# A projection done alone: both weight pieces taken at once, all wide products with hi before all products with lo

## The chip, the cores and the metric

The kernel runs on one core of one Trainium2 chip. The metric is device time in microseconds (us) of one launch, the median of several runs. Before the change it is 2928.85 us (3 runs, 2928.5 to 2928.92). One more execution was taken with the hardware profiler; it took 2928.61 us, and its profile spans 2926.8 us.

## What is computed

The reference is a two-layer decoder trunk over 256 tokens of width 2048, in float32. Layer 0 mixes with a convolution group and a differential-attention group that share one input and one output projection, layer 1 with a short gated convolution. After its mixer each layer cross-attends with 4 heads of 512 into 256 memory tokens, and applies an MLP of width 8192 with squared ReLU. Cut to what matters here:

```
x = x + even_mixer(rms(x))  or  x + odd_mixer(rms(x))   # in: D -> 5*1024 or 3*2048; out: 2048 -> 2048
x = x + softmax((rms(x) @ wq) @ (mem @ wk).T) @ (mem @ wv) @ wo
x = x + square(relu(rms(x) @ w1)) @ w2                  # 2048 -> 8192 -> 2048
```

Nearly all the work is `act @ weight` with 256 rows of `act`, and each weight is used once.

## The kernel before

**Split numbers.** Every float32 operand is split in two: `hi`, rounded to the format that TensorE takes in one pass, and `lo`, what is left of it. A product is hi\*hi + lo\*hi + hi\*lo. Activations lie in `Act` objects: for each of 16 chunks of 128 channels, 256 columns of hi and 256 columns of lo side by side. `act.both(k)` is all 512 columns, `act.hi(k)` the first 256.

**Weights.** `weights(src)` (lines 152 to 165) brings one piece of 128 x 1024: SyncE issues the transfer into `raw` (5 buffers), ScalarE casts it to `whi` (line 163, 3 buffers), VectorE subtracts to get `wlo` (line 164, 3 buffers). A projection to 128 output channels reads 16 chunks, so two such pieces, `g = 0` and `g = 1`, of 8 blocks of 128 x 128 each.

**A projection alone.** `proj(src, act)` does one projection with one PSUM bank `mm` (4 buffers) through `proj_group`. In its wide form each piece is handled by `wide_piece` (lines 173 to 182): the hi blocks times `act.both` (512 columns: hi\*hi in the left half of the bank, hi\*lo in the right), then the lo blocks times `act.hi` (256 columns, left half). In the last piece the eighth hi block is kept back and closes the bank. So TensorE gets, for one projection, 8 products of 512 columns, 8 of 256, 7 of 512, 8 of 256, 1 of 512. Afterwards ScalarE copies the right half and VectorE adds it to the left (`summed`, lines 205 to 210), or VectorE adds both halves to the residual (`residual`, line 324). The narrow form (`wide=False`, products of 256 columns alone) serves the convolution inputs and the memory keys; `proj_rows` serves the values; `proj_group` with 3 or 4 sources serves the first output columns of `even_out` and `xo`.

**Who calls proj in its wide form.** The q and k of the differential attention (16), `even_out` (13), `odd_in` (48), `odd_out` (16), the cross-attention's q (32) and `xo` (24), and the MLP (256).

**The order of the work.** The framework orders each engine's instructions from its own plan, mostly by their order in the program. Two things are fixed by hand. While `strict[0]` is set (even mixer, and the cross-attention from its first query chunk to its first four output columns), all products go to TensorE in the program's order (`ordered(i, "pe")`). The `wlo` subtractions and the convolution taps on VectorE keep the program's order too. Work of the attention is placed by due times that are counted in calls of `weights`: `stage(delay, fn)` notes `fn` for `delay` calls later, and each call of `weights` first runs what is due (`run_stages`, line 154) and then counts itself:

```
run_later(rate[0], calls[0])
run_stages(calls[0])
calls[0] += 1
```

In the cross-attention (lines 642 to 710), a head's four query chunks are projected with `proj`, scaled and split into `xq` (lines 698 to 701), and then `stage(X0, scores)` with `X0, X1, X2 = 1, 2, 1`. `scores` does 24 products `sx` of 256 columns (for each half of the rows four chunks i, each with q hi, q lo, q hi), and the softmax; `turn` transposes 2 calls later; `heads_out` multiplies with the values 1 call after that. The differential attention has the delays `D0, D1, D2, D3 = 2, 3, 2, 2` for scores, transposes, output and the mean of squares; its heads come in pairs, two wide projections a head, followed by two pairs of narrow projections (`gated`).

Of the kernel before, what the change touches and what calls it, by code (L numbers as in the profile page):

```python
# [10 lines left out]
F32 = mybir.dt.float32  # L11
# [6 lines left out]
P = 128  # L18
D = 2048
S = 256  # L20
# [25 lines left out]
def trunk(ctx: ExitStack, tc: tile.TileContext, d):  # L46
# [11 lines left out]
    ps_mm = ctx.enter_context(tc.tile_pool(name="ps_mm", bufs=4, space=bass.MemoryType.PSUM))  # L58
# [3 lines left out]
    def f(ap):  # L62
        return ap.bitcast(F32)
# [55 lines left out]
    def ordered(i, token):  # L119

        tc.stamp_issue_order_token(i.ins, token)
# [7 lines left out]
    def run_later(n, upto):  # L129
        while n and background and background[0][0] <= upto:  # L130
            background.pop(0)[1]()
            n -= 1

    def run_stages(upto):
        while True:
            due = [e for e in stages if e[0] <= upto]
            if not due:
                return
            stages.remove(due[0])
            due[0][1]()  # L140

    def mm(*a, **k):
        i = T.matmul(*a, **k)  # L143
        if strict[0]:
            ordered(i, "pe")
# [6 lines left out]
    def weights(src):  # L152
# [3 lines that stand above are left out]
        raw = wraw.tile([P, 1024], F32, tag="raw", name="raw")  # L156
        hi = wspl.tile([P, 1024], F32R, tag="whi", name="whi")
        lo = wspl.tile([P, 1024], F32R, tag="wlo", name="wlo")
        n = 512 if calls[0] == 1 else 1024
        for i in range(0, 1024, n):  # L160
            o = slice(i, i + n)
            nc.sync.dma_start(out=raw[:, o], in_=src[:, o])
            A.copy(hi[:, o], raw[:, o])  # L163
            ordered(V.tensor_tensor(lo[:, o], raw[:, o], f(hi[:, o]), op=ALU.subtract), "lo")  # L164
        return hi, lo

    def block(ps, hi, lo, act, k, first, last):

        mm(ps, hi, act.hi(k), start=first, stop=False)
        mm(ps, hi, act.lo(k), start=False, stop=False)  # L170
        mm(ps, lo, act.hi(k), start=False, stop=last)

    def wide_piece(ps, hi, lo, act, k, first, last):


        w = [slice(j * P, (j + 1) * P) for j in range(8)]
        for j in range(7 if last else 8):
            mm(ps, hi[:, w[j]], act.both(k + j), start=first and j == 0, stop=False)
        for j in range(8):
            mm(ps[:, :S], lo[:, w[j]], act.hi(k + j), start=False, stop=False)  # L180
        if last:
            mm(ps, hi[:, w[7]], act.both(k + 7), start=False, stop=True)

    def proj_group(srcs, act, order=(0, 1), wide=True):


        pp = [ps_mm.tile([P, 512], F32, tag="mm", name="mm")[:, :(2 * S if wide else S)] for _ in srcs]
        for g in order:
            if g == order[-1] and len(srcs) > 1:
                run_stages(END)  # L190
            for src, ps in zip(srcs, pp):
                hi, lo = weights(src[:, g * 1024:(g + 1) * 1024])
                first, last = g == order[0], g == order[-1]
                if wide:
                    wide_piece(ps, hi, lo, act, g * 8, first, last)
                    continue
                for j in range(8):
                    w = slice(j * P, (j + 1) * P)
                    block(ps, hi[:, w], lo[:, w], act, g * 8 + j, first and j == 0, last and j == 7)
        return pp  # L200

    def proj(src, act, wide=True):
        return proj_group([src], act, wide=wide)[0]

    def summed(ps):
# [145 lines left out]
    def even_mixer():  # L351
# [37 lines left out]
        def qk(c, hl, name, sign):  # L389
            t = summed(proj(w[2 * NA + c], xa))  # L390
            V.scalar_tensor_tensor(t, t, sign, r, op0=ALU.mult, op1=ALU.mult)
            A.copy(hl[:, 0], t)
            V.tensor_tensor(hl[:, 1], t, f(hl[:, 0]), op=ALU.subtract)
            return hl
# [94 lines left out]
        def gated(c):  # L489
            pv = proj(w[c], xa, wide=False)  # L490
            av = tmp32("av")
            V.tensor_tensor(av, pv, r, op=ALU.mult)
            pg = proj(w[NA + c], xa, wide=False)
            ag = tmp32("ag")
            V.tensor_tensor(ag, pg, r, op=ALU.mult)
            A.activation(ag, ag, AF.Sigmoid)
            V.tensor_tensor(a[:, c], av, ag, op=ALU.mult)
            i = c * CK
            def tap(c=c, i=i, j=CK - 1):
                s = CK - 1 - j  # L500
                if not s:
                    ordered(V.tensor_scalar(cv[:, c], a[:, c], col("conv_a_w", i + j), col("conv_a_b", c),
                                            op0=ALU.mult, op1=ALU.add), "lo")
                else:
                    ordered(V.scalar_tensor_tensor(cv[:, c, s:], a[:, c, :S - s], col("conv_a_w", i + j),  # L505
                                                   cv[:, c, s:], op0=ALU.mult, op1=ALU.add), "lo")

            def total(c=c):
                if c == 0:
                    V.tensor_copy(lsum, cv[:, 0])  # L510
                else:
                    V.tensor_tensor(lsum, lsum, cv[:, c], op=ALU.add)

            for j in range(CK - 1, -1, -1):
                later(lambda tap=tap, j=j: tap(j=j))
            later(total)
# [60 lines left out]
        for c, ps in enumerate(proj_group([d["even_out"][c] for c in range(3)], cat, (1, 0))):  # L577
            residual(c, ps, nxt, nss, "xat0")
# [63 lines left out]
    def cross(l, xa, ss, kmem):  # L642
# [62 lines left out]
        for c, ps in enumerate(proj_group([d[f"xo{l}"][c] for c in range(4)], oa)):  # L705
            residual(c, ps, nxt, nss, f"mlp{l}")
# [96 lines left out]
```

## Time and profile before

| quantity | before |
|---|---|
| median of 3 runs | 2928.85 us |
| the profiled execution's own time | 2928.61 us |
| its span in the profile | 2926.8 us |
| mean granted TensorE clock | 0.998 |
| TensorE matmul (PE) busy | 2907.2 us, 99% |
| TensorE weight load (PEld) busy | 2583.8 us, 88% |
| VectorE (DVE) busy | 2000.0 us, 68% |
| ScalarE (ACT) busy | 1456.8 us, 50% |
| DMA | 540.12 MB, mean 185 GB/s |

PE and PEld are two rows for the same engine: PE the products, PEld the loads of the 128 x 128 block, which run ahead of them. Products are pipelined, so the time that one product costs isn't its listed duration but the distance from its start to the start of the next one; where below a number is called a pitch, this is meant. In a timeline the columns are start (us), duration of the group, engine, line, operation, output<-inputs, number of instructions, and in brackets the engine's idle time before it with what ended it.

### The profile page before, as it was taken

How to read it: one execution, taken by the hardware profiler on the slowest of the kernel's cores; microseconds unless marked ns; L12 is line 12 of the kernel's file. 1: busy time of each engine (PE TensorE's matmuls, PEld its weight loads, DVE VectorE, ACT ScalarE, POOL GpSimd, SP SyncE). 2: the span in 40 equal slices, each digit the busy share in tenths (PEclk: the TensorE clock that was granted, in tenths of full speed). 3: DMA queues.
4: the chain of work that ended last, by engine and by line, in shares of the span. 5: the costliest groups of instructions: out<-in, count | busy, mean ns of one | idle time of the engine just before them, and what ended most of it. 6: DMA issues, size and time to landing. Idle time of an engine off the chain costs nothing.

```text
span 2926.8 us, 44172 instructions
## 1 busy us (share of the span) xinstructions
PE 2907.2 (99%) x17304; PEld 2583.8 (88%) x17304; DVE 2000.0 (68%) x3132; ACT 1456.8 (50%) x2133; POOL 3.9 (0%) x20
## 2 busy tenths in 40 slices
PE   9999999999999999999999999999999999999998
PEld 7999988898888888888888899888988888888887
DVE  7899987767666656666777764467676666566665
ACT  6665455555544535445544443455555445354453
POOL 0000000000000000000000000000000000000000
PEclk9999999999999999999999999999999999999999
DMA  7454565545565665666655655655455656656564
GB/s 249 163 191 167 180 187 188 171 151 178 184 191 187 190 187 187 189 190 190 182 192 197 202 191 187 192 189 170 142 188 183 191 188 189 189 190 188 188 188 136
DMA packets 150401, 540.12 MB, mean 185 GB/s; under 512 B 16688, under 2 KB 16816, under 8 KB 150192
## 3 DMA queue, kind: packets, MB, share of 16 engines
q1 hardware_dynamic: 150192, 537.30, 58.0%
q8 instruction: 136, 2.23, 0.3%
q14 instruction: 73, 0.60, 0.1%
HBM read 535.13 MB, written 2.10 MB: 184 GB/s over the span
## 4 chain that ended last, share of the span: by engine, by line
PE 99%; DVE 0%; DMA 0%; ACT 0%; issue 0%; DVEq 0%; SPq 0%; ACTq 0%
PE mm L143 89%; PE mmr L143 8%; PE pox L143 1%; PE sx L143 1%; PE nmb L143 0%; PE sc L143 0%; PE nmr L143 0%; PE po L143 0%; DVE x L741 0%; PE ptx L148 0%; DMA x<-xT 0%; PE ptd L148 0%; ACT xn L254 0%; DVE x L324 0%; DVEq L798 0%
## 5 line engine op out<-in xcount | busy, mean ns | idle before, releaser
L163 ACT CAST whi<-raw 128x1024 fp32r<-128x1024 f32 (+1 forms) x1009 | 1060.3, 1051 | 829.4 <-PE mm L143 702.2
L164 DVE TENSOR_TENSOR wlo<-raw,whi 128x1024 fp32r<-128x1024 f32 (+1 forms) x1009 | 1233.6, 1223 | 278.4 <-ACT whi L163 260.5
L143 PE MATMUL mm<-xn,whi 128*128 128x512 f32 (+1 forms) x4096 | 997.5, 379 | 0.0
L143 PEld LDWEIGHTS mm<-xn,whi 128*128 128x128 f32 x4096 | 724.7, 189 | 115.6
L143 PE MATMUL mm<-xn,wlo 128*128 128x256 f32 x3840 | 572.9, 282 | 0.0
L143 PEld LDWEIGHTS mm<-xn,wlo 128*128 128x128 f32 x3840 | 537.8, 190 | 34.7
L143 PE MATMUL mm<-hid,whi 128*128 128x512 f32 x2048 | 514.1, 392 | 0.0
L143 PEld LDWEIGHTS mm<-hid,whi 128*128 128x128 f32 x2048 | 368.9, 189 | 65.9
L208 ACT COPY sum<-mm 128x256 f32<-128x256 f32 x224 | 83.4, 372 | 533.0 <-PE mm L143 532.8
L324 DVE TENSOR_TENSOR x<-x,mm 128x256 f32<-128x256 f32 x384 | 161.5, 421 | 265.9 <-PE mm L143 259.2
L209 DVE TENSOR_TENSOR sum<-mm,sum 128x256 f32<-128x256 f32 x224 | 95.0, 424 | 313.2 <-ACT sum L208 312.7
L143 PEld LDWEIGHTS mm<-hid,wlo 128*128 128x128 f32 x2048 | 279.4, 190 | 19.9
L143 PE MATMUL mm<-hid,wlo 128*128 128x256 f32 x2048 | 285.6, 282 | 0.0
L143 PE MATMUL mm<-mem,whi 128*128 128x256 f32 x1024 | 185.4, 284 | 0.0
L143 PEld LDWEIGHTS mm<-mem,whi 128*128 128x128 f32 x1024 | 158.8, 190 | 0.0
L143 PE MATMUL mm<-mem,wlo 128*128 128x256 f32 x512 | 144.9, 283 | 0.0
L143 PE MATMUL mmr<-whi,mem 128*128 128x512 f32 x512 | 137.3, 390 | 0.0
L143 PE MATMUL mm<-o,whi 128*128 128x512 f32 x512 | 129.3, 393 | 0.0
L505 DVE SCALAR_TENSOR_TENSOR cv<-a,vec,cv 128x255 f32<-128x255 f32 (+14 forms) x240 | 111.5, 465 | 3.4
L143 PEld LDWEIGHTS mmr<-whi,mem 128*128 128x128 f32 x512 | 95.7, 188 | 19.5
L143 PEld LDWEIGHTS mm<-o,whi 128*128 128x128 f32 x512 | 92.2, 189 | 17.3 <-DVE o L251 0.9
L143 PEld LDWEIGHTS mm<-mem,wlo 128*128 128x128 f32 x512 | 97.4, 190 | 0.0
(165 smaller groups left out, 1803.6 us busy)
## 6 DMA issues: line engine op xcount, KB each, us to landing
raw<-w SPq DMA_DIRECT2D x512, 512.0 KB, 4.1
raw<-odd_in SPq DMA_DIRECT2D x96, 512.0 KB, 4.6
raw<-even_in SPq DMA_DIRECT2D x64, 512.0 KB, 4.4
raw<-xk SPq DMA_DIRECT2D x64, 512.0 KB, 3.7
raw<-xv SPq DMA_DIRECT2D x64, 512.0 KB, 3.5
raw<-xq SPq DMA_DIRECT2D x64, 512.0 KB, 3.9
raw<-xo SPq DMA_DIRECT2D x64, 512.0 KB, 3.8
raw<-even_out SPq DMA_DIRECT2D x32, 512.0 KB, 4.3
```

What stands on the lines that cost most here:

```text
L143: i = T.matmul(*a, **k)
L163: A.copy(hi[:, o], raw[:, o])
L164: ordered(V.tensor_tensor(lo[:, o], raw[:, o], f(hi[:, o]), op=ALU.subtract), "lo")
L208: A.copy(t, ps[:, S:])
L209: V.tensor_tensor(t, ps[:, :S], t, op=ALU.add)
L324: V.tensor_tensor(x[:, k], x[:, k], ps[:, i * S:(i + 1) * S], op=ALU.add)
L505: ordered(V.scalar_tensor_tensor(cv[:, c, s:], a[:, c, :S - s], col("conv_a_w", i + j), cv[:, c, s:], op0=ALU.mult, op1=ALU.add), "lo")
```

## The change

`proj` in its wide form no longer goes through `proj_group`, but through a new function `proj_long`. It calls `weights` for both pieces first, and then gives TensorE 15 products of 512 columns with the hi blocks, 16 of 256 columns with the lo blocks, and one of 512 columns that closes the bank. The products are the same 32 on the same operands; their order, and the place of the second call of `weights` in the program, are different. Narrow projections, `proj_rows` and `proj_group` with several sources are as they were.

```
+    def proj_long(src, act):
+        ps = ps_mm.tile([P, 512], F32, tag="mm", name="mm")
+        (h0, l0), (h1, l1) = [weights(src[:, g * 1024:(g + 1) * 1024]) for g in range(2)]
+        w = [slice(j * P, (j + 1) * P) for j in range(8)]
+        for k in range(15):
+            mm(ps, (h0, h1)[k // 8][:, w[k % 8]], act.both(k), start=k == 0, stop=False)
+        for k in range(16):
+            mm(ps[:, :S], (l0, l1)[k // 8][:, w[k % 8]], act.hi(k), start=False, stop=False)
+        mm(ps, h1[:, w[7]], act.both(15), start=False, stop=True)
+        return ps
...
     def proj(src, act, wide=True):
+        if wide:
+            return proj_long(src, act)
         return proj_group([src], act, wide=wide)[0]
```

## The prediction

> **What bounds the kernel now.** I read the page first: busy times, the chain that ended last, and the two groups of rows that tell how many wide projections there are.
>
> ```profile
> span 2926.8 us, 44172 instructions
> ...
> PE 2907.2 (99%) x17304; PEld 2583.8 (88%) x17304; DVE 2000.0 (68%) x3132; ACT 1456.8 (50%) x2133; POOL 3.9 (0%) x20
> ...
> PE 99%; DVE 0%; DMA 0%; ACT 0%; issue 0%; DVEq 0%; SPq 0%; ACTq 0%
> ...
> L208 ACT COPY sum<-mm 128x256 f32<-128x256 f32 x224 | 83.4, 372 | 533.0 <-PE mm L143 532.8
> L324 DVE TENSOR_TENSOR x<-x,mm 128x256 f32<-128x256 f32 x384 | 161.5, 421 | 265.9 <-PE mm L143 259.2
> ```
>
> TensorE is the bound from end to end. Any pitch that gets shorter comes straight off the time, and any gap goes straight onto it. L208 runs once per `summed` projection (224), L324 twice per residual one (192, of which the groups with several sources hold 3 + 4 + 4). So 224 + 181 = **405** projections go the new way.
>
> Then the waits of TensorE's weight loads, longest first:
>
> ```profile
> PEld mmr L143 <- ACT whi L163: 6.1, 1, 6.1
> PEld nmb L143 <- ACT diag L273: 4.3, 6, 2.9
> ...
> PEld mm L143 <- DVE o L251: 0.9, 2, 0.4
> PEld mmr L143 <- DVE wlo L164: 0.5, 2, 0.3
> ```
>
> Outside the start and the end of the kernel TensorE hardly waits: weights are in time throughout. What is left is the pitch itself, so I took the timeline of the products in the MLP, from one closing product (x1) to one 80 projections later, and one long stretch of 512-column products with nothing else between (10 groups of 4 and 2).
>
> ```profile
> 1004.75 0.40 PE L143 MATMUL mm<-xn,whi 128*128 128x512 f32 x1
> 1004.98 2.00 PE L143 MATMUL mm<-hid,whi 128*128 128x512 f32 x8
> 1006.82 1.12 PE L143 MATMUL mm<-hid,wlo 128*128 128x256 f32 x8
> 1007.77 1.78 PE L143 MATMUL mm<-hid,whi 128*128 128x512 f32 x7
> 1009.38 1.12 PE L143 MATMUL mm<-hid,wlo 128*128 128x256 f32 x8
> ...
> 1451.68 0.40 PE L143 MATMUL mm<-hid,whi 128*128 128x512 f32 x1
> ```
> ```profile
> 1004.75:1451.68 446.93, 446.93 (x2562) 393.30 (x2561) 284.09 (x382) 211.83 (x289) 0.00 (x0) 1.00 0.62 189
> ```
> ```profile
> 1843.46 1.07 PE L143 MATMUL mmr<-whi,mem 128*128 128x512 f32 x4
> ...
> 1857.06 0.39 PE L143 MATMUL mmr<-whi,mem 128*128 128x512 f32 x1
> ```
> ```profile
> 1843.46:1857.06 13.60, 13.60 (x61) 1.00 0.66 193
> ```
>
> One projection takes 446.93 / 80 = 5.587 us. The undisturbed pitch of 512 columns is 13.60 / 60 = 0.2267 us. That of 256 columns is 0.120: 24 products `sx` from 556.78 to 559.66, rows below. Sixteen of each make 5.547, so 0.040 of each projection is lost to something. The timeline shows where: 8 hi products take 1.84 where 8 pitches are 1.813, 7 take 1.61 for 1.587, and the lo runs take 0.95 and 0.96 for 0.96. The loss comes with the switch from 256 to 512 columns, some 0.025 a run, and is over by the seventh product (the eighth costs 1.84 - 1.61 = 0.23); the lo runs give back about 0.005.
>
> **The change, part by part.**
>
> *Fewer switches.* Each projection has two hi runs and two lo runs now, one of each after. The loss is halved: 0.020 us less each, 405 x 0.020 = **-8.1 us**. The bounds are 0 (if the loss belongs to the piece and not to the switch) and -16.2 (if long runs lose nothing); I take the half, since the rows show the loss in the first seven products of a run and nothing behind them.
>
> [...]
>
> *Due work moves ahead of whole projections.* Both calls of `weights` now come before the first product. Work due at the first call stands where it stood; work due at the second call, which used to come between the two pieces, now comes before the projection. For the cross-attention this moves `scores`: it is registered with delay 1 after a head's fourth query chunk and is due at the second call of the next projection. Today one piece (8 hi and 8 lo products) lies between the fourth chunk and its scores; after the change nothing does. These are the rows of head 0:
>
> ```profile
> 553.76 2.23 PE L143 MATMUL mm<-xn,whi 128*128 128x512 f32 x9
> 554.20 0.37 ACT L208 COPY sum<-mm 128x256 f32<-128x256 f32 x1 [2.23 <-PE mm L143]
> 554.47 1.06 ACT L163 CAST whi<-raw 128x1024 fp32r<-128x1024 f32 x1
> 554.60 0.42 DVE L209 TENSOR_TENSOR sum<-mm,sum 128x256 f32<-128x256 f32 x1 [1.51 <-ACT sum L208]
> 555.06 0.42 DVE L699 TENSOR_TENSOR sum<-sum,rb 128x256 f32<-128x256 f32 x1
> 555.52 0.41 ACT L700 CAST xq<-sum 128x256 fp32r<-128x256 f32 x1
> 555.56 1.23 DVE L164 TENSOR_TENSOR wlo<-raw,whi 128x1024 fp32r<-128x1024 f32 x1
> 555.83 1.12 PE L143 MATMUL mm<-xn,wlo 128*128 128x256 f32 x8
> ...
> 556.70 0.42 DVE L701 TENSOR_TENSOR xq<-sum,xq 128x256 fp32r<-128x256 f32 x1
> 556.78 3.04 PE L143 MATMUL sx<-hl,xq 128*128 128x256 f32 x24
> ...
> 559.66 0.63 PE L143 MATMUL mm<-xn,whi 128*128 128x512 f32 x2
> ```
>
> The x9 row begins with the closing product at 553.76. From there the chain is copy, add, scale, cast, subtract; the lo part of the query is there at 557.12, that is 3.36 us after the closing product started. The subtraction stands behind a weight subtraction of 1.23 us on VectorE, which was ready earlier. After the change the scores start one pitch (0.23) behind the closing product. The first nine use chunks 0 to 2, which are long there, the tenth the cast hi of chunk 3, the eleventh its lo. The eleventh would start at 0.23 + 10 x 0.120 = 1.43. How late it starts once VectorE is done is seen where TensorE waits for `o`:
>
> ```profile
> 657.03 2.07 PE L143 MATMUL mm<-o,whi 128*128 128x512 f32 x7
> 657.85 0.69 DVE L251 TENSOR_TENSOR o<-pox,o 128x512 fp32r<-128x512 f32 x1 [0.75 <-ACT o L250]
> 658.94 0.28 PE L143 MATMUL mm<-o,wlo 128*128 128x256 f32 x1
> ```
>
> Seven hi products take 1.91 here against 1.61; the last, due at 657.03 + 6 x 0.23 = 658.41, is 0.30 late, so counts from 658.71, 0.17 after VectorE's end at 658.54. The gap in the scores is 3.36 + 0.17 - 1.43 = 2.10 us. It comes for heads 0, 1, 2 of both layers (head 3's scores fall into the group of four `xo` columns, which keeps its pieces apart): 6 x 2.10 = **+12.6 us**. TensorE is in the hand-written order there, so the next projection's 15 hi products queue behind the gap, and nothing can fill it. The lower bound is 1.37 a head (the query's subtraction goes ahead of the weights': 555.93 - 553.76 + 0.04 + 0.42 + 0.17 - 1.43), the upper 3.33 (a second weight subtraction of 1.23 ahead of it). I take 2.10, because VectorE takes what is ready and the weight cast still ends before the query's cast.
>
> The stages behind keep or gain cover: `turn` comes two calls later, still a whole projection (5.57) behind the scores, `heads_out` now a projection behind `turn` and not a piece. In the differential attention the scores fall due at a first call (k of the next head) or among narrow projections, which are unchanged. Only the mean of squares of every second head moves ahead of a q projection; one narrow piece of 24 products (2.9 us) still covers its square. Cost 0; without that cover 0.4 us (a copy such as L208 takes 372 ns), three times, 1 us.
>
> *Weight buffers.* The second `whi` is wanted earlier (from the ninth product on), and its `wlo` may be written only when the first eight lo products of the projection before are done. That leaves it one projection, 5.57 us, for a subtraction of 1.23; up to now it was three pieces less the lo run, 3 x 2.79 - 0.95 = 7.4. The cover is the MLP's idle VectorE (284 of 447 us busy) and, in the heads of the even mixer, what these rows leave:
>
> ```profile
> 45.00:340.00 295.00, 295.00 (x2229) 280.48 (x2228) 265.67 (x603) 175.57 (x325) 1.87 (x6) 1.00 0.54 178
> ```
> ```profile
> 116.25 1.23 DVE L164 TENSOR_TENSOR wlo<-raw,whi 128x1024 fp32r<-128x1024 f32 x1
> ...
> 123.22 1.11 PE L143 MATMUL mm<-xn,wlo 128*128 128x256 f32 x8
> ```
>
> VectorE is 90% busy; counted through in order, the wide piece subtracted until 117.48 is the one used from 123.22, so 5.7 us of slack shrink by at most 1.8. Cost 0. Without it, 16 q and k projections would wait; at the 0.3 us that TensorE's longest wait for `wlo` took, that is 4.8 us. Count and order of the transfers on SyncE's queue stay the same, with five raw buffers ahead of them: 0.
>
> **Sum.** -8.1 + 12.6 = +4.5 us. On the profiled execution's own 2928.61 that is 2933.1; it lies 0.24 below the median of the runs, so the median becomes **2933.3** (+0.15%).
>
> **The rivals.**
>
> 1. *Short gap.* The query's subtraction goes first: 6 x 1.37 = 8.2, less 8.1: 2928.9. For it: the plan may order VectorE anew. Against: the lo subtraction stands ahead in the rows above.
> 2. *No gap*, the change does just what it says: -8.1, 2920.7. It needs the scores to find their query ready. Against: due times decide, and the rows show `sx` exactly one piece after the closing product.
> 3. *The loss belongs to something else than the switch* (to a new pair of weight tiles, say): no gain, only the gaps, 2928.85 + 12.6 = 2941.4, slower. For it: every switch here is also a change of tile. Against: the long stretch changes tiles too, at 0.2267. [...]
> 4. *VectorE comes late in the heads*, slower: the in-order queue, held by a `wlo` whose buffer frees 1.8 us later, passes the delay to TensorE in 16 projections: +4.8 on the forecast, 2938.1. It decides once the slack of 5.7 falls under zero. For it: 90% busy. Against: 1.8 is less than 5.7.
>
> **How the numbers follow.** Forecast 52%, short gap 20%, no gap 10%, no gain 8%, late VectorE 10%. About 0.2%, 5.9 us, is what a measurement can tell from no change; the forecast's +4.5 lies near it, and one in five of its cases (gaps above 2.3 us) goes over. Slower: 8 + 10 + 10 = 28%. Faster: the 10 of no gap and 2 from an even shorter gap than the short one, 12%. Within: 60%. The range goes from the no-gap case to the late VectorE, 2920.5 to 2938.5, and leaves out the no-gain case and the farthest of the late one.
>
> **What would show it.** Timeline in the MLP: one run of 16 hi and one of 16 lo, 5.567 us a projection; 5.587 refutes the first step. In the list of waits, TensorE's loads waiting for `xq` L701, six times, about 2 us each (for L700 first, shortly); none would refute the second. `sx` directly behind a closing product. No waits for `wlo` from 45 to 340 us. A time below 2925 or above 2937 would say that one of the two terms is not there.

## The result and the profile after

The changed kernel takes 2935.2 us (median of 12 runs, 2932.95 to 2936.21) against 2928.61 us before (12 runs, 2928.13 to 2929.28). The ratio is 1.0021, 95% interval 1.0012 to 1.0029: slower by 6.6 us. The forecast was 2933.3. The runs spread over 3.3 us after and 1.2 before. The profiled execution is at the upper end of its runs, 2936.21 us.

The page of the changed kernel, busy times and the groups that read PSUM or make the weights:

```profile
span 2934.4 us, 44173 instructions
...
PE 2905.4 (99%) x17304; PEld 2588.2 (88%) x17304; DVE 1995.2 (68%) x3132; ACT 1456.4 (50%) x2133; POOL 3.9 (0%) x20
...
L164 DVE TENSOR_TENSOR wlo<-raw,whi 128x1024 fp32r<-128x1024 f32 (+1 forms) x1009 | 1235.0, 1224 | 784.0 <-issue 350.2
...
L339 DVE TENSOR_TENSOR x<-x,mm 128x256 f32<-128x256 f32 x384 | 160.7, 418 | 14.6 <-PE mm L143 7.9
```

TensorE is still the bound, 99% busy before and after, with as many products (17304). VectorE's idle time has moved. These are the weight subtraction's row in the page of the kernel before, and what VectorE waited for ahead of it in the changed one:

```profile
L164 DVE TENSOR_TENSOR wlo<-raw,whi 128x1024 fp32r<-128x1024 f32 (+1 forms) x1009 | 1233.6, 1223 | 278.4 <-ACT whi L163 260.5
```
```profile
DVE wlo L164 <- issue: 350.2, 245, 1.8
DVE wlo L164 <- PE mm L143: 260.0, 140, 3.7
```

Before, 278.4 us stood ahead of the subtraction and 265.9 ahead of the residual additions; now it is 784.0 and 14.6. Of the 784.0, 260.0 us ended with products of TensorE, which fits a wait for a `wlo` buffer that they still read; for 350.2 us the profile names no cause ("issue"). Whether any of it costs time is seen in TensorE's own waits, the loads' list of the changed kernel:

```profile
PEld mmr L143 <- ACT whi L163: 6.3, 1, 6.3
PEld sx L143 <- DVE xq L716: 6.0, 6, 1.0
PEld sx L143 <- ACT xq L715: 5.7, 6, 0.9
...
PEld mmr L143 <- DVE wlo L164: 0.2, 1, 0.2
```

Two rows are new, six times each: the scores wait for the query's hi part and then for its lo part. No lone projection waits for weights. The timeline of TensorE in the MLP, and of head 0's scores:

```profile
1010.39 0.40 PE L143 MATMUL mm<-xn,whi 128*128 128x512 f32 x1
1010.62 3.58 PE L143 MATMUL mm<-hid,whi 128*128 128x512 f32 x15
1014.04 2.08 PE L143 MATMUL mm<-hid,wlo 128*128 128x256 f32 x16
...
1455.72 0.40 PE L143 MATMUL mm<-hid,whi 128*128 128x512 f32 x1
```
```profile
552.98 0.40 PE L143 MATMUL mm<-xn,whi 128*128 128x512 f32 x1
553.22 1.24 PE L143 MATMUL sx<-hl,xq 128*128 128x256 f32 x9
...
554.74 0.41 ACT L715 CAST xq<-sum 128x256 fp32r<-128x256 f32 x1
554.77 1.23 DVE L164 TENSOR_TENSOR wlo<-raw,whi 128x1024 fp32r<-128x1024 f32 x1
...
555.20 0.38 PE L143 MATMUL sx<-hl,xq 128*128 128x256 f32 x1 [0.74 <-ACT xq L715]
555.91 0.42 DVE L716 TENSOR_TENSOR xq<-sum,xq 128x256 fp32r<-128x256 f32 x1
556.38 1.93 PE L143 MATMUL sx<-hl,xq 128*128 128x256 f32 x14 [0.80 <-DVE xq L716]
...
558.15 2.23 PE L143 MATMUL mm<-xn,whi 128*128 128x512 f32 x9
```

Eighty projections take 445.33 us, 5.567 each, against 5.587. The scores follow the closing product directly; nine products run, the tenth waits for the cast, the eleventh for the subtraction that stands behind a weight subtraction. From 553.22 to 558.15 are 4.93 us for 24 products that take 24 x 0.120 = 2.88: a gap of 2.05 us.

Both terms of the sum are there, close to their sizes. What the sum lacks is in the windows view: the granted clock (the share of full clock that TensorE was given, third number from the end) in stretches of the changed kernel. The stretches are as long as a fall of the clock, 3.41 us, and laid end to end from one; such a stretch is called a window below. The last two of the rows lie behind the gaps of head 1 in layer 0 and head 0 in layer 1.

```profile
583.58:586.99 3.41, 1.87 (x13) 1.00 0.45 171
2017.18:2020.59 3.41, 1.87 (x13) 1.00 0.55 185
2078.62:2082.03 3.41, 1.92 (x13) 1.00 0.53 178
552.86:556.27 3.41, 1.98 (x14) 1.00 0.52 185
```
```profile
587.02:590.38 3.36, 3.36 (x15) 3.36 (x16) 1.19 (x5) 0.57 (x2) 0.00 (x0) 0.50 0.50 172
2020.61:2024.00 3.39, 3.39 (x13) 2.91 (x12) 1.61 (x6) 1.13 (x4) 0.00 (x0) 0.50 0.35 122
```

Behind two of the six gaps TensorE runs for 3.41 us at half clock. The four rows of the upper view are the windows that hold most of a gap: the first two, 1.87 us busy, are followed by half clock, the other two, 1.92 and 1.98 busy, are not. (The last two of the six gaps left their windows 2.08 us busy or more, and the clock stayed whole.) What a stretch at half clock costs is seen from the starts of the scores in layer 0. Head 0's stand above, at 553.22; these are those of heads 1 and 2, again in TensorE's timeline of the changed kernel:

```profile
583.76 1.24 PE L143 MATMUL sx<-hl,xq 128*128 128x256 f32 x9
...
615.84 1.24 PE L143 MATMUL sx<-hl,xq 128*128 128x256 f32 x9
```

From head 0 to head 1 it is 30.54 us with a gap, from head 1 to head 2 it is 32.08 with a gap and half clock: 1.54 us a stretch. In the profiled execution the span grew by 7.6 us. Six gaps of 2.05 and two stretches of 1.54 make 15.4, so by this count the new order gained the other 7.8.

### The profile page after: what moved, and what is told of

It is laid out like the page before. It is cut to its first block, busy times and chain, and to the rows that moved or that the text cites. A ratio compares the mean times of both kernels' runs of the same rounds, so it can differ in the third digit from the quotient of the medians.

```text
span 2934.4 us, 44173 instructions
## 1 busy us (share of the span) xinstructions
PE 2905.4 (99%) x17304; PEld 2588.2 (88%) x17304; DVE 1995.2 (68%) x3132; ACT 1456.4 (50%) x2133; POOL 3.9 (0%) x20
## 4 chain that ended last, share of the span: by engine, by line
PE 99%; DVE 1%; ACT 0%; DMA 0%; issue 0%; DVEq 0%; SPq 0%; ACTq 0%
PE mm L143 89%; PE mmr L143 8%; PE pox L143 1%; PE sx L143 1%; PE nmb L143 0%; DVE wlo L164 0%; PE sc L143 0%; PE nmr L143 0%; ACT whi L163 0%; PE po L143 0%; DVE x L756 0%; DMA x<-xT 0%; PE ptx L148 0%; PE ptd L148 0%; DVE xq L716 0%
## 5 line engine op out<-in xcount | busy, mean ns | idle before, releaser
L164 DVE TENSOR_TENSOR wlo<-raw,whi 128x1024 fp32r<-128x1024 f32 (+1 forms) x1009 | 1235.0, 1224 | 784.0 <-issue 350.2
L143 PE MATMUL mm<-xn,whi 128*128 128x512 f32 (+1 forms) x4096 | 959.4, 378 | 0.0
L143 PEld LDWEIGHTS mm<-xn,whi 128*128 128x128 f32 x4096 | 739.9, 189 | 127.9
L143 PE MATMUL mm<-xn,wlo 128*128 128x256 f32 x3840 | 537.8, 283 | 0.0
L143 PEld LDWEIGHTS mm<-xn,wlo 128*128 128x128 f32 x3840 | 508.6, 191 | 17.4
L143 PE MATMUL mm<-hid,whi 128*128 128x512 f32 x2048 | 489.8, 391 | 0.0
L143 PEld LDWEIGHTS mm<-hid,whi 128*128 128x128 f32 x2048 | 377.0, 188 | 72.8
L143 PEld LDWEIGHTS mm<-hid,wlo 128*128 128x128 f32 x2048 | 262.6, 191 | 9.9
L143 PE MATMUL mm<-hid,wlo 128*128 128x256 f32 x2048 | 265.7, 283 | 0.0
L339 DVE TENSOR_TENSOR x<-x,mm 128x256 f32<-128x256 f32 x384 | 160.7, 418 | 14.6 <-PE mm L143 7.9
```

The source lines that it names most:

```text
L339: V.tensor_tensor(x[:, k], x[:, k], ps[:, i * S:(i + 1) * S], op=ALU.add)
```

## The experiments

Two theories went in. **A**: the cost is the gaps, plus half clock that gaps bring on when enough of one falls into one window. **B**: the gaps cost their length, and the rest of the loss comes from the new order itself, such as weights that come late.

**Give the scores their cover back**, everything else as changed.

```
-            stage(X2, lambda: heads_out(h, pb, v))
+            stage(X2 if h == XH - 1 else X2 + 1, lambda: heads_out(h, pb, v))
...
-            stage(X0, lambda h=h, q=q, k=k: scores(h, q, k))
+            stage(X0 if h == XH - 1 else X0 + 1, lambda h=h, q=q, k=k: scores(h, q, k))
```

> The changed kernel, but for heads 0 to 2 of each layer the scores are due one call later (delay 2 in place of 1) and so is the output stage, so that a whole projection lies between the last query chunk and its scores. Theory A (what the change costs is the six gaps in the scores, plus stretches at half clock that these gaps bring on): no gaps, no half clock, 2928.6 - 7.8 = 2920.8 us, and runs within 0.6 us of each other. Theory B (the gaps cost 12.3, and the 3 us beyond the sum come from something else that the new order brings, such as late weights): 2923.6 or more. If switches do not matter: 2928.6.

Measured: 2921.58 us (2920.95 to 2922.25, 9 runs), ratio 0.9976 (0.9967 to 0.9986). TensorE's timeline in this kernel, and a new wait in the lists of its loads and of its products:

```profile
558.32 0.40 PE L143 MATMUL mm<-xn,whi 128*128 128x512 f32 x1
558.55 3.04 PE L143 MATMUL sx<-hl,xq 128*128 128x256 f32 x24
561.43 0.86 PE L143 MATMUL mm<-xn,whi 128*128 128x512 f32 x3
```
```profile
PEld ptx L148 <- DVE pexp L674: 1.0, 1, 1.0
```
```profile
PE ptx L148 <- DVE pexp L674: 0.7, 1, 0.7
```

The 24 products take 2.88 us, no clock falls before the end (mean granted clock 0.998), and the kernel beats the one before by 7.1 us. Of the 0.8 us by which it misses theory A, most is explained by one head's transposes, which now wait for their softmax: 1.0 us in the loads' list, 0.7 in the products'. The changed kernel doesn't have this wait. B's 2923.6 is out: no cost of the new order beside the gaps is seen.

**Fill part of each gap with useless work.** Eight products whose result nobody reads stand ahead of the scores of heads 0 to 2.

```
+            if h < XH - 1:
+                fill = ps_at.tile([P, 512], F32, tag="at", name="fill")[:, :S]
+                for n in range(8):
+                    mm(fill, xa.hi(n)[:, :P], xa.hi(n), start=n == 0, stop=n == 7)
```

> The changed kernel with 8 products of 256 columns, whose result nobody reads, put ahead of the scores of heads 0 to 2 of each layer: they take 0.96 us out of each gap of 2.05 us, and TensorE's total loss stays the same. Theory A: no stretch at half clock any more, 2928.6 - 7.8 + 12.3 = 2933.1 us, and a narrower spread than the 3.3 us of the changed kernel (below 1 us). Theory B: as the changed kernel, 2935.2 us, with the same spread.

Measured: 2933.5 us (2932.98 to 2934.1, 11 runs). TensorE's timeline of this kernel:

```profile
553.76 1.12 PE L143 MATMUL fill<-xn 128*128 128x256 f32 x8
554.72 1.41 PE L143 MATMUL sx<-hl,xq 128*128 128x256 f32 x10
556.92 1.94 PE L143 MATMUL sx<-hl,xq 128*128 128x256 f32 x14 [0.80 <-DVE xq L720]
558.71 3.59 PE L143 MATMUL mm<-xn,whi 128*128 128x512 f32 x15
```

From the first filler to the next projection it is 4.95 us, where the changed kernel has 4.93. TensorE loses as much, and yet the kernel is 1.7 us quicker, and its runs spread over 1.1 us (just above the 1 expected) and not 3.3. The trace has no half clock between the start and the end of the kernel (mean granted clock 0.998). So six gaps that were in part filled with useless products cost 1.7 us less here than six idle ones of the same length (2933.5 against 2935.2); the two traces differ in the half clock, none here and two stretches in the changed kernel.

**How little filling is enough?** The same with 2 products, so that each gap shrinks only to 1.81 us.

> The changed kernel with 2 products of 256 columns, whose result nobody reads, ahead of the scores: the gaps of 2.05 us become 1.81 us. If the stretches at half clock need about 1.95 us of idle time in one window (what the profile of the changed kernel suggests: 1.97 brought one on, 1.92 did not): none any more, 2933.3 us with a spread under 1.2 us. If any gap of this kind can do it: 2934.5 to 2935.5 us with a spread of 3 us.

Measured: 2933.35 us (2932.61 to 2934.21, 11 runs). The trace has no half clock between the start and the end of the kernel (mean granted clock 0.998). The runs spread over 1.6 us, more than the 1.2 expected, and as much as the 25 runs of the kernel before that were taken beside the first experiments (1.56). In the two traces half clock followed two of the six gaps of 2.05 us and none of the six of 1.81.

**Lengthen the gaps.** In the changed kernel the scores begin with the late chunk.

```
-                for i in range(4):
+                for n, i in enumerate((3, 0, 1, 2)):
```

> The changed kernel, but the scores begin with query chunk 3, the late one, so that each of the six gaps is some 3.1 us and not 2.05. If a gap brings on a stretch at half clock whenever some 2 us of idle time fall into one window of 3.41 us (theory A): four to six stretches of 1.55 us, 2928.6 - 7.8 + 6 x 3.13 + 7.5 = 2947 us (2945.5 to 2949). If half clock needs a whole idle window, which 3.1 us cannot fill: no stretches, 2939.6 us.

Measured: 2946.98 us (2946.22 to 2951.6, 4 runs). The waits, the window of head 0's gap and what follows it, a window of head 1's gap and its successor, and the other three falls of the clock:

```profile
PEld sx L143 <- ACT xq L715: 12.8, 6, 2.1
PEld sx L143 <- DVE xq L716: 6.6, 8, 1.0
```
```profile
554.77:558.14 3.37, 1.45 (x10) 1.00 0.56 180
558.21:561.61 3.40, 3.40 (x17) 0.50 0.35 127
585.51:588.92 3.41, 1.69 (x14) 1.00 0.52 174
588.93:592.33 3.40, 2.52 (x19) 1.00 0.68 241
623.06:626.46 3.40, 3.40 (x17) 0.50 0.34 123
2025.94:2029.34 3.40, 3.40 (x18) 0.50 0.41 145
2090.79:2094.19 3.40, 3.40 (x19) 0.50 0.39 145
```

The first window was busy for 1.45 us and half clock followed all the same, so here it came without a whole idle window; four of six gaps brought it on in this execution. But the window of 1.69 us was not followed by half clock, though windows of 1.87 were in the changed kernel: the listed busy time can't be what decides (the last section comes back to it). One of the four runs took 2951.6 us, above the expected 2949, at a mean granted clock of 0.994 where the others have 0.996; it left no trace, and why it lost more stays open.

**The old order with both calls first.** The products go back to 8 hi, 8 lo, 7 hi, 8 lo, 1 hi; the two calls of `weights` stay ahead.

```
-        for k in range(15):
...
+        wide_piece(ps, h0, l0, act, 0, True, False)
+        wide_piece(ps, h1, l1, act, 8, False, True)
```

> Both weight pieces are called for first, as in the changed kernel, but the products keep their old order (8 hi, 8 lo, 7 hi, 8 lo, 1 hi). Theory A: the gain of fewer switches goes, the gaps and the half clock stay: 2928.6 + 12.3 + 3 = 2944 us, between 2941 and 2947, with a spread of some us. If the gain of 7.8 came from taking both pieces at once and not from the order of the products: 2935 us.

Measured: 2942.53 us (2941.03 to 2943.24, 4 runs), ratio 1.0047 (1.0033 to 1.006). TensorE's timeline in the MLP of this kernel:

```profile
1010.81 0.40 PE L143 MATMUL mm<-xn,whi 128*128 128x512 f32 x1
...
1457.74 0.40 PE L143 MATMUL mm<-hid,whi 128*128 128x512 f32 x1
```

Eighty projections take 446.93 us, to the hundredth what they took before the change. So the gain is the order's alone, and taking both pieces at once, with the due times as they stand, brings only loss. The profiled execution (2942.44 us) has one stretch at half clock; 2928.7 + 12.3 + 1.5 gives 2942.5.

**Only the due time, in the kernel before.** Nothing of the change, but the scores come one call sooner (and their transposes one call later behind them, where they were).

```
-            stage(X1, lambda: turn(h, pr, v))
+            stage(X1 if h == XH - 1 else X1 + 1, lambda: turn(h, pr, v))
...
-            stage(X0, lambda h=h, q=q, k=k: scores(h, q, k))
+            stage(X0 if h == XH - 1 else 0, lambda h=h, q=q, k=k: scores(h, q, k))
```

> The kernel before, with one due time changed: the scores of heads 0 to 2 of each layer come at the next call (delay 0, transposes one later to stay where they are), so that they follow the last query chunk directly. Nothing of the change is in it. Theory A (gaps and half clock cost the same whatever the order of the products): 2928.6 + 12.3 + 1 to 4 of half clock = 2942 to 2945 us, with a spread of over 1.5 us. If the gaps hurt only in the new order: 2929 to 2933 us.

Measured: 2943.32 us (2941.15 to 2944.68, 4 runs), ratio 1.0047 (1.0031 to 1.0062). TensorE's timeline of this kernel shows the same two waits at the tenth and the eleventh product:

```profile
556.55 0.38 PE L143 MATMUL sx<-hl,xq 128*128 128x256 f32 x1 [0.74 <-ACT xq L700]
557.73 2.95 PE L143 MATMUL sx<-hl,xq 128*128 128x256 f32 x14 [0.80 <-DVE xq L701]
```

The loss of the change can be had without the change, from the due times alone.

**Call for the second piece between the hi products**, so that due work stands behind the first eight.

```
+        h0, l0 = weights(src[:, :1024])
...
+            if k == 8:
+                h1, l1 = weights(src[:, 1024:2048])
```

> The new order of the products, but the second weight piece is called for after the first eight hi products, so that work due at the second call stands behind those 8 products (1.84 us) and not ahead of the projection. Theory A: a gap of about 2.05 - 1.84 = 0.2 us a head, six of them, no half clock: 2928.6 - 7.8 + 1.3 = 2922.1 us. Theory B: 2925 us.

Measured: 2922.64 us (2921.93 to 2923.18, 10 runs), ratio 0.9979 (0.997 to 0.9988). In its list of waits:

```profile
PEld sx L143 <- DVE xq L718: 1.1, 6, 0.2
```

Six gaps of 0.2 us are left, as 1.84 us of cover against 2.05 leave. This edit too turns the change into a gain, by the new order with the due times as they were; it lies 0.5 us above theory A and well below B's 2925.

**Fewer switches still.** On top of the first experiment every second lone projection turns its order around.

```
+        flip[0] = not flip[0]
+        front = 15 if flip[0] else 1
+        for k in range(front):
...
+        for k in range(front, 16):
```

> As e1_scores_later, and every second lone projection begins with one hi product, then 16 lo, then 15 hi, so that two projections share runs of 30 hi and of 2 hi in place of two runs of 16. Theory A (the loss is paid at the entry of a run of 512 columns, 6 + 9 + 1 + 5 + 4 ns over its first five products, and a run of lo gives 7 ns back): 11 ns less per two projections, 202 times: 2921.6 - 2.2 = 2919.4 us. If the lo weights are wanted too early and come late: 2922 us or more, with waits for wlo.

Measured: 2919.28 us (2919.01 to 2919.74, 5 runs), ratio 0.9967 (0.9955 to 0.998). Rows of TensorE's timeline of this kernel, the last one 15 pairs of projections behind the first, and a new row in the loads' list:

```profile
1012.84 2.08 PE L143 MATMUL mm<-hid,wlo 128*128 128x256 f32 x16
1014.75 0.63 PE L143 MATMUL mm<-hid,whi 128*128 128x512 f32 x2
1015.22 2.06 PE L143 MATMUL mm<-hid,wlo 128*128 128x256 f32 x16
...
1179.44 2.08 PE L143 MATMUL mm<-xn,wlo 128*128 128x256 f32 x16
```
```profile
PEld mm L143 <- ACT hid L264: 2.7, 8, 0.3
```

Two hi products take 0.47 us, of which 0.453 are two pitches: the short run pays 0.016 of the 0.027 that a run of five or more pays (by the trace's starts in nanoseconds). The kernel gains 2.3 us over the first experiment, and the sum said 2.2, but that it agrees is luck. A pair of projections takes (1179.44 - 1012.84) / 15 = 11.107 us here against 2 x 5.567, so 0.027 less and not 0.011: the sum took every lo run to give back 0.007, and behind a run of two hi products it gives back 0.022. For 202 pairs that would be 5.4 us. The eight new waits for `hid`, 2.7 us in the loads' list, take part of it back; the rest isn't accounted for. The kernel is the fastest of all, 9.5 us below the kernel before.

## Why the prediction was right, and what it lacked

- *Fewer switches, -8.1 us.* Right. 5.567 us a projection was forecast and measured, and putting the old order back restored 5.587. Without gaps the whole kernel gained 7.1, and up to 1.0 more if the transposes' new wait is taken off. The hi runs of 16 change their weight tile behind the ninth product, and in the trace the tenth costs no more than its pitch (0.2267 us, the mean of the MLP's 80 runs of 16), so a new tile alone isn't what costs here.
- *Gaps in the scores, 6 x 2.10 = +12.6 us.* Right in place, number and cause, a little large: 2.05 each. The query's subtraction ended at 556.33, 3.35 us after the closing product's start (forecast 3.36). The link behind it was mis-sized: the eleventh product started 0.05 after VectorE's end, not 0.17, and the 14 products from there took 0.09 more than their pitches (556.38 to 558.15). The kernel with two fillers, which loses the same time, stands at 2933.35 against the first experiment's 2921.58: 11.8, and up to 12.8 if that experiment's own wait is taken off it.
- *Weight buffers, 0.* Right for the time. VectorE did come to stand idle ahead of line 164, for 784.0 us, of which 260.0 ended with products of TensorE, but TensorE waited for no weights of a lone projection: the slack that was counted covered it. The rival of a late VectorE fell with that.
- *The differential attention, the output stage and the mean of squares, 0.* TensorE's list of waits has no new row for them.
- *The sum, +4.5 us.* Here a term was missing. The sum took a gap to cost its length. Two of the six in the profiled execution also cost the clock behind them, 1.54 us a stretch. The two terms that were there stand at 12.3 and -7.8 by the count above, each some 0.3 smaller than forecast, and that this cancels is luck. Both kernels with fillers, which have the gaps' price without the clock's, lie within 0.3 us of the forecast (2933.5 and 2933.35 against 2933.3); the changed kernel lies 1.9 above it. At 1.54 us a stretch that is between one and two (1.2) in a typical run; the profiled one had two. That is an estimate from the times alone: one stretch changes a run's mean granted clock by 0.0006, too little for the listed clocks to count them (0.997 for the two slowest of the twelve runs, 0.998 for the other ten). The forecast held because the missing term is small beside its range, not because it was thought of.
- *The chances.* The forecast gave 28% to slower by over 0.2%, and the measured 0.21% to 0.23% falls there, just over the border that the forecast's +4.5 was said to lie near (the interval, 0.12% to 0.29%, has the border in it). The missing term carried it over; the 28% was not given for that, but for longer gaps, no gain or a late VectorE. Of the rivals, the short gap, no gap and no gain are out: line 164 did go ahead of line 716, the gaps are there, and so is the gain.
- *The signs.* The wait of the scores came as two, 0.9 for the cast and 1.0 for the subtraction, not one of about 2.

## What to carry to other kernels

When work is placed by counting calls, moving a call moves everything that is due at it: list what falls due there, and ask for each item what covered it. A gap on the busiest engine has to be priced with what follows it, here a clock that was halved for 3.41 us behind two of six gaps, 1.54 us a stretch. Where the gap couldn't be avoided, some useless products in it were cheaper here than idling (2933.35 and 2933.5 us against 2935.2). And where products of two widths alternate, the switches themselves can be counted and saved: half of them were worth 0.020 us a projection here (5.567 against 5.587).

## What was not expected of the hardware

In the changed kernel the granted clock was halved for 3.41 us behind two of the six gaps of 2.05 us. Between the start and the end of a kernel the traces have nine such stretches, each listed at 3413 ns: two in the changed kernel, one in the old order with both calls first, two in the kernel before with the due time alone, and four in the kernel that begins with the late chunk. In this last one the falls at 558.20 and 623.05 us, and those at 2025.93 and 2090.78, lie 64.85 us apart, which is 19 x 3.413; in the changed kernel the two at 587.00 and 2020.59 lie 1433.60 us apart, which is 420 x 3.4133. So the falls of one trace stand whole windows apart, and how much of a gap lies in one window differs from gap to gap.

The falls of the changed kernel go with the time that a window is without products, if each product is counted with its pitch, 0.227 us for 512 columns and 0.120 for 256. The window from 583.58 to 586.99 holds 0.16 us of a closing product's pitch, ten score products of 0.120 and 0.08 us of the run that follows the gap: 1.44 us, and 1.97 without. Counted so, the windows that hold most of the six gaps are without products for 2.07 and 1.97 us, with half clock behind them, and for 1.92, 1.86, 1.76 and 1.28 us, without it. The listed busy time blurs this, because the last product before each wait is listed with its whole duration (0.38 us for the one at 555.20). The window of 1.69 us busy in the kernel that begins with the late chunk has few such products: 1.53 us by pitches, 1.88 without, and no fall. A gap of 2.05 us thus cost 2.05 or 3.6 us here, which fits the spread of 3.3 us of the changed kernel's runs, of which one left a trace.
